# Output gate rows by one matmul with ones, a PSUM bank moved in stage 1, and new costs in the order's planner

## The chip, the cores and the metric

The kernel runs on one core of one Trainium2 chip. The metric is the device time of one execution in microseconds (us); lower is better. Engines are named as in the profile: PE (TensorE), DVE (VectorE), ACT (ScalarE), POOL (GpSimd, which here only issues DMAs) and SP (SyncE, which issues the weight loads).

## What is computed

One layer of a diffusion backbone in float32, with 256 latent tokens, 256 context tokens and a model width of 4096. All weight matrices are read once from DRAM. Shortened from the reference:

```python
shift_x, scale_x, gate_x = modulation(c, w_ada[l], b_ada[l])      # silu(c) @ w_ada + b_ada, 3 x 4096
shift_c, scale_c, gate_c = modulation(c_ctx, w_ada[l], b_ada[l])
h_x = rmsnorm(x, norm_w[l]) * (1.0 + scale_x[:, None]) + shift_x[:, None]
h_c = rmsnorm(ctx, norm_w[l]) * (1.0 + scale_c) + shift_c
q_x, k_x, v_x, ga_x, xl_x, gl_x = jnp.split(h_x @ w_in[l], SPLITS, axis=-1)
q_c, k_c, v_c, ga_c, xl_c, gl_c = jnp.split(h_c @ w_in[l], SPLITS, axis=-1)
# attention of 16 query heads over 512 keys (4 kv heads, QK norm, rotary positions)   -> att_x
# convolution of width 4, gates, one scan per direction over 16 blocks of 128 channels -> lru_x
mix_x = jnp.concatenate([rmsnorm(att_x, out_norm_att[l]) * jax.nn.silu(ga_x),
                         rmsnorm(lru_x, out_norm_lru[l]) * jax.nn.silu(gl_x)], axis=-1)
x_new = x + gate_x[:, None] * (mix_x @ w_out[l])
```

The change concerns `gate_x`, the output gate: 4096 numbers, one for each output column, that multiply the output projection.

## The kernel before

**Arithmetic.** A large matrix product is three float32r matmuls: each operand is split into a rounded high part and the rest. ACT casts a weight tile to its high part (L688, `hi`), DVE subtracts to get the low part (L692, `lo`), and PE does high by high, low by high and high by low (L789 to L791 in stage 1, L1007 to L1009 after). A piece is two weight rows of 128, so six matmuls of 128x128 by 512 columns. There are seven raw weight slots (`raw`), three `hi` and three `lo` slots.

**Stage 1** goes over the 32 tiles of 128 input channels in groups of 1, 1, 2, 2, 2 and then 4. For each group the modulation (shift and scale of both streams) is made from `w_ada`, partly by PE (`on_tensor`, L525) and partly by DVE (`on_vector`, L515, two products for each weight row of 128), then turned (`coeff_tasks`, a bank of class `pe`). The token tiles are transposed by PE into a `pe` bank (`turn`, L639), and ACT reads that bank four times to make high part and full value (`modulate`, L649 and L650); DVE makes the low part from the single `ta` buffer. Then come the columns that both streams need, key, value and recurrence input, in six blocks of 512 columns. The four token tiles (two latent, two context) of a block fill one PSUM bank each, of class `pm`; when a group is through a block, DVE adds each bank to an SBUF accumulator (L809) and the bank is free. The eight banks of PSUM are four `pm`, two `pe`, one `pt`, one `po`.

**Stage 2** makes the query blocks, attention, the recurrence and the two SiLU gates, **stage 3** the output projection in eight chunks of 512 columns, each multiplied by its gate and added to `x` by DVE and stored by POOL's queue. `Q0` is the end of stage 1 and `O0` the start of stage 3; a chunk (`CH`) is 192 large matmuls.

**Output gate.** Row j covers 512 columns. DVE adds 32 products of a weight row with a column of `silu(c)` in one accumulator `ga` (L914; L912 for the first one), so that each partition holds a partial sum. For rows 0 to 3 four matmuls with a column of ones (L927) sum over partitions into four columns of `gT`, DVE adds the bias (L931), and in stage 3 four matmuls with the identity (L1518) and an ACT copy (L1522) spread them again over 128 partitions. Rows 4 to 7 have the bias as one row of the first addend (L921, L922), are summed and spread by one matmul with a matrix of ones (L937, `spread`), and ACT copies them to an SBUF tile (L942, `keep`).

**Order.** Tiles are placed by hand. Each step is a task with an engine, a cost, what it depends on and which buffers it takes and frees. A planner (`Plan`) simulates the engines with those costs and so fixes one order for all; each engine's queue then follows it strictly. POOL's DMAs are one in-order queue in the plan (engine "S"), SP's weight loads are issued in the order in which they are used, as slots come free. A cost or a bank count that is changed in the plan therefore re-deals the order everywhere.

Of the kernel before, what the change touches and what calls it, by code (L numbers as in the profile page):

```python
# [55 lines left out]
PICK = 0.10  # L56
MOD_VPOS = 2.7
NCONST = 128 + 2 + 4 * 128


class Task:


    def __init__(self, fn, ops, deps=(), pos=0.0, nb=None, loads=(), frees=0, acq=(), rel=()):
        self.fn, self.ops, self.deps = fn, ops, [d for d in deps if d is not None]
        self.pos, self.nb, self.loads, self.frees = pos, nb, loads, frees
        self.acq, self.rel = acq, rel
        self.start = self.end = self.arrived = None
# [10 lines left out]
def pe(n, k=1):  # L79
    return k * n / 2400  # L80
# [12 lines left out]
class Plan:  # L93
# [23 lines left out]
    def estimate(self, t):  # L117
        s = self.t[t.ops[0][0]]
        for d in t.deps:
            s = max(s, d.end + (0.0 if d.ops[-1][0] == t.ops[0][0] else self.LAT[d.ops[-1][0]]))  # L120
        need = {}
        for n in t.acq:
            need[n] = need.get(n, 0) + 1
        for n, c in need.items():
            f = sorted(self.free[n])
            if len(f) < c:
                return None
            s = max(s, f[c - 1] + 0.1)
# [90 lines left out]
def kernel(  # L219
# [34 lines left out]
    SLOTS = dict(h4=(22, 1024), a8=(6, 2048), raw=(RAW, 1024), hi=(HL, 1024), lo=(HL, 1024), tp=(TP, 512), ta=(1, 512), wg=(2, 514),  # L254
                 xin=(1, 512), u=(1, 512), ga=(1, 512), ab=(2, 16), cf=(1, 16), mx=(3, 2), ss=(5, 16), pm=(4, 512), pe=(2, 512), pt=(1, 512), po=(1, 512))
    ROUNDED = ("h4", "hi", "lo")
# [69 lines left out]
    epsc = cp.tile([128, 1], F32, name="epsc")  # L326
    ones_c = cp.tile([128, 1], F32, name="ones_c")
    par_t = slot("xin", [128, 512])
# [12 lines left out]
    V.memset(pick[:, 3:4], 1.0)  # L341
    V.memset(ones_c, 1.0)
    V.memset(par[:, 0], 0.0)
# [20 lines left out]
    rope = {}  # L364
    gT = cp.tile([128, KT], F32, name="gT")
    st = cp.tile([128, 4, NG], F32, name="st")
# [310 lines left out]
    def unit(w_l, k0, kw, c0, cw, pos):  # L677

        u = len(units)
        shape = [128, kw, cw]  # L680
        src = w_l[128 * k0 : 128 * (k0 + kw), c0 : c0 + cw].rearrange("(k p) n -> p k n", p=128)
        d = dict(pos=pos)
        units.append(d)

        def high(raw):
            d["raw"] = raw
            d["hi"] = slot("hi", shape, F32R)
            S.copy(d["hi"], raw)  # L688

        def low():  # L690
            d["lo"] = slot("lo", shape, F32R)
            V.tensor_tensor(out=d["lo"], in0=d["raw"], in1=d["hi"].bitcast(F32), op=ALU.subtract)  # L692
            drop(d["raw"])

        before = units[u - 1] if u else {}
        p = pos - AHEAD
        d["high"] = add(high, [("A", act(1024))], [before.get("high")], p, nb=pos - 40, loads=[(shape, src)], acq=["hi"])
        d["low"] = add(low, [("D", dve(1024))], [d["high"], before.get("low")], p, frees=1, acq=["lo"])
        return u
# [31 lines left out]
    def accum_task(name, tile_, fn, dep, pos):  # L731
# [3 lines left out]
        deps = [dep, summed.get((name, tile_)), acc_last.get(name)]  # L735
        acc_last[name] = summed[name, tile_] = add(fn, ops, deps, pos, acq=acq, rel=["pm"])

# [160 lines left out]
    WHOLE = 4  # L898
    gbias, wide = {}, {}

    def gate_tasks(j, prev, lru_read=None):

        d = {}
        src = w_ada[0, :, 2 * D + 512 * j : 2 * D + 512 * j + 512].rearrange("(p k) n -> p k n", p=128)

        def mul(w, k):
            if k == 0:
                d["acc"] = slot("ga", [128, 512])
            for i in range(2):
                s_ = sc[:, 0, k + i : k + i + 1]  # L910
                if k + i == 0 and j < WHOLE:
                    V.tensor_scalar_mul(d["acc"], w[:, i], s_)  # L912
                else:
                    V.scalar_tensor_tensor(out=d["acc"], in0=w[:, i], scalar=s_, in1=d["acc"] if k + i else gbias["row"], op0=ALU.mult, op1=ALU.add)  # L914
# [24 lines left out]

        def keep():  # L940
            gb = h4t([128, 512])
            S.copy(gb, d["pg"])  # L942
            drop(d["pg"])
            wide[j] = gb

        if j >= WHOLE:
            if j == WHOLE:
                prev = add(row, [("D", 0.3)], [lru_read, prev], gate_pos(16 * j) - 8, acq=["xin"])
            else:
                prev = add(row, [("S", 0.05, 6.0)], [prev], gate_pos(16 * j) - 1)  # L950
        for k in range(0, KT, 2):
            pos = gate_pos(16 * j + k // 2)
            prev = add(lambda w, k=k: mul(w, k), [("D", 1.33)], [prev], pos, nb=pos - GATE_EARLY, loads=[([128, 2, 512], src[:, k : k + 2])], frees=1,
                       acq=["ga"] if k == 0 else [])
        if j >= WHOLE:
            a = add(spread, [("P", 1.05)], [prev], pos, acq=["pe"], rel=["ga"])
            gate_fin.append(add(keep, [("A", act(512))], [a], pos, acq=["h4"], rel=["pe"]))
            return prev
        a = add(sums, [("P", 0.8)], [prev], pos, acq=["pe"], rel=["ga"])
        gate_fin.append(add(fin, [("D", 0.1)], [a], pos, rel=["pe"]))  # L960
        return prev

# [5 lines left out]

    gated = None
    for j in range(WHOLE):  # L970
        gated = gate_tasks(j, gated)

# [73 lines left out]

    ROTATE = dve(128, 4) + dve(512, 2)
    res = {}
# [419 lines left out]
    def make_post():  # L1468
# [20 lines left out]
    for n in range(NB):  # L1489
        prev = lru_tasks(n, Q0 + 0.9 * CH + span * n, span, prev)  # L1490
    for j in range(WHOLE, 8):
        gated = gate_tasks(j, gated, prev["cv"])

# [12 lines left out]
    for j in range(8):  # L1506
# [6 lines left out]

        def turn(d=d, j=j):
            d["pg"] = bank()
            for i in range(4):
                n = 4 * j + i
                T.matmul(d["pg"][:, 128 * i : 128 * i + 128], gT[:, n : n + 1].to_broadcast([128, 128]), ident, start=True, stop=True)  # L1518

        def put(d=d):  # L1520
            d["gb"] = slot("tp", [128, 512])
            S.copy(d["gb"], d["pg"])  # L1522
            drop(d["pg"])

        def scaled(t, d=d, j=j):
            o = d["ps"][t]
            if j >= WHOLE:
                d["gb"] = wide[j]
            for c in (slice(0, 256), slice(256, 512)) if j == 7 else (slice(0, 512),):
# [12 lines left out]
        if j < WHOLE:  # L1542
            a = add(turn, [("P", pe(2048))], [gb], p + 0.85 * CH, nb=p + 0.5 * CH, acq=["pe"])
            gb = add(put, [("A", act(512))], [a], p + 0.87 * CH, acq=["tp"], rel=["pe"])
        d["ps"], ends = rows_pieces(o_units[j], mh, lambda g: [mixed[g]])
        for t in range(2):
            a = add(lambda t=t, f=scaled: f(t), [("D", dve(512, 2))], [ld, gb, ends[t]], p + CH, rel=["pm"] + ([["tp"], ["h4"]][j >= WHOLE] if t else []))
            add(lambda t=t, f=store: f(t), [("S", 0.73)], [a], p + CH, rel=["a8"] if t else [])
# [51 lines left out]
```

## Time and profile before

| | |
|---|---|
| median of 3 runs | 1749.03 us (1748.51 to 1751.44) |
| the profiled execution | 1748.74 us |
| its span | 1747.0 us |
| PE busy | 1694.0 us, 97% of the span |
| PE weight load busy | 1305.3 us, 75% |
| DVE busy | 1393.2 us, 80% |
| ACT busy | 854.0 us, 49% |
| DMA | 451.23 MB, 258 GB/s in the mean |
| large matmuls | 768 of each line in stage 1, 1280 of each line after |

Times in the trace are from the start of the span. Of PE, the start times tell more than the busy time: matmuls are pipelined and their records overlap. An "idle before" in brackets at a row is the time its engine had been without work, and who ended it. Stage 1's large matmuls start from 34.5 to 706.8 us, those of stages 2 and 3 from 707.5 to 1740.8 us.

### The profile page before, as it was taken

The numbers are of one execution on the slowest core, as the hardware profiler recorded it, in microseconds if no ns is written. First come the engines' busy times: TensorE is split into PE (matmuls) and PEld (weight loads), VectorE is DVE, ScalarE is ACT, GpSimd is POOL, SyncE is SP. The second block draws the span as 40 slices with busy tenths as digits, with TensorE's granted clock in tenths as the row PEclk, the third lists the DMA queues.
The fourth block names the chain that finished last, engine by engine and source line by source line (L and its number), as shares of the span: only waits on it lengthen the run. The fifth ranks groups of instructions, "written<-read, shape, count | busy, mean of one in ns | idle before, by whom it ended". The sixth has DMA issues, their size and how long they took to land.

```text
span 1747.0 us, 22544 instructions
## 1 busy us (share of the span) xinstructions
PE 1694.0 (97%) x8133; PEld 1305.3 (75%) x8133; DVE 1393.2 (80%) x1998; ACT 854.0 (49%) x1254; POOL 60.5 (3%) x97
## 2 busy tenths in 40 slices
PE   4999999999999999999999999999999999999998
PEld 2556677777676778877777778888888788888887
DVE  2368888898988897597886779989987988786874
ACT  5422232232323233366886877777687643343332
POOL 0000000000000000000000000000000000000000
PEclk9999999999999999999999999999999999999999
DMA  9999988889787875885544538767876799898983
GB/s 320 333 354 327 352 297 279 298 298 318 249 319 276 284 254 164 269 260 185 189 127 125 153 119 294 219 222 232 266 237 202 225 338 324 289 327 284 332 290 103
DMA packets 253104, 451.23 MB, mean 258 GB/s; under 512 B 14976, under 2 KB 56560, under 8 KB 252480
## 3 DMA queue, kind: packets, MB, share of 16 engines
q1 hardware_dynamic: 246624, 428.43, 73.9%
q0 software_dynamic: 6368, 21.36, 3.5%
q8 instruction: 64, 1.05, 0.2%
q14 instruction: 48, 0.39, 0.1%
HBM read 441.34 MB, written 8.39 MB: 257 GB/s over the span
## 4 chain that ended last, share of the span: by engine, by line
PE 56%; DVE 23%; DMA 10%; issue 5%; ACT 5%; SPq 1%; DVEq 0%; ACTq 0%
PE pm L1009 11%; PE pm L1007 11%; PE pm L1008 11%; DMA raw<-in_w_ada_dram 8%; DVE lo L692 7%; PE pm L789 5%; PE pm L790 5%; PE pm L791 5%; DVE u L515 3%; DVE xin L515 2%; ACT hi L688 2%; DMA raw<-in_w_in_dram 2%; DVE ga L914 1%; DVE a L809 1%; PE pt L525 1%
## 5 line engine op out<-in xcount | busy, mean ns | idle before, releaser
L688 ACT CAST hi<-raw 128x1024 fp32r<-128x1024 f32 x416 | 435.6, 1050 | 684.8 <-PE pm L1009 284.0
L692 DVE TENSOR_TENSOR lo<-raw,hi 128x1024 fp32r<-128x1024 f32 x416 | 506.6, 1221 | 178.5 <-ACT hi L688 175.8
L1007 PE MATMUL pm<-hi,h 128*128 128x512 f32 x1280 | 514.8, 402 | 0.0
L1008 PE MATMUL pm<-lo,h 128*128 128x512 f32 x1280 | 499.4, 390 | 2.0 <-DVE lo L692 1.9
L1009 PE MATMUL pm<-hi,h 128*128 128x512 f32 x1280 | 499.6, 390 | 0.0
L789 PE MATMUL pm<-hi,h 128*128 128x512 f32 x768 | 313.8, 409 | 9.1 <-DVE a L809 7.7
L790 PE MATMUL pm<-lo,h 128*128 128x512 f32 x768 | 301.5, 393 | 0.8 <-DVE lo L692 0.8
L791 PE MATMUL pm<-hi,h 128*128 128x512 f32 x768 | 301.5, 393 | 0.0
L1008 PEld LDWEIGHTS pm<-lo,h 128*128 128x128 f32 x1280 | 240.8, 188 | 55.8 <-issue 5.3
L1007 PEld LDWEIGHTS pm<-hi,h 128*128 128x128 f32 x1280 | 240.6, 188 | 52.2 <-issue 5.3
L1009 PEld LDWEIGHTS pm<-hi,h 128*128 128x128 f32 x1280 | 240.4, 188 | 50.7
L789 PEld LDWEIGHTS pm<-hi,h 128*128 128x128 f32 x768 | 145.0, 189 | 82.1 <-issue 28.9
L914 DVE SCALAR_TENSOR_TENSOR ga<-raw,sc,ga 128x512 f32<-128x512 f32 x248 | 185.8, 749 | 5.6 <-DMA raw<-in_w_ada_dram 0.8
L791 PEld LDWEIGHTS pm<-hi,h 128*128 128x128 f32 x768 | 145.1, 189 | 31.6
L790 PEld LDWEIGHTS pm<-lo,h 128*128 128x128 f32 x768 | 145.4, 189 | 27.6 <-DVE lo L692 1.3
L809 DVE TENSOR_TENSOR a<-pm,a 128x512 f32<-128x512 f32 x202 | 133.0, 686 | 35.4 <-PE pm L791 35.1
L515 DVE SCALAR_TENSOR_TENSOR xin<-raw,sc,xin 128x512 f32<-128x512 f32 (+1 forms) x188 | 135.7, 722 | 24.6 <-DMA raw<-in_w_ada_dram 24.6
L515 DVE SCALAR_TENSOR_TENSOR u<-raw,sc,u 128x512 f32<-128x512 f32 (+1 forms) x188 | 135.8, 722 | 0.0
L525 PE MATMUL po<-raw,wg 128*32 128x256 f32 (+2 forms) x560 | 55.9, 473 | 26.1 <-DMA raw<-in_w_ada_dram 26.0
L525 PEld LDWEIGHTS po<-raw,wg 128*32 128x32 f32 x560 | 15.6, 120 | 55.1 <-DMA raw<-in_w_ada_dram 21.9
L649 ACT ACTIVATE ta<-pe,ab 128x256 f32<-128x256 f32 x64 | 36.1, 564 | 42.4 <-PE pe L639 31.1
L525 PE MATMUL pt<-raw,wg 128*32 128x512 f32 (+2 forms) x456 | 42.8, 466 | 4.1 <-DMA raw<-in_w_ada_dram 3.9
(198 smaller groups left out, 1295.4 us busy)
## 6 DMA issues: line engine op xcount, KB each, us to landing
raw<-in_w_ada_dram SPq DMA_DIRECT2D x384, 512.0 KB, 5.9
raw<-in_w_in_dram SPq DMA_DIRECT2D x288, 512.0 KB, 4.6
raw<-in_w_out_dram SPq DMA_DIRECT2D x128, 512.0 KB, 5.1
h<-in_x_dram SPq DMA_DIRECT2D x8, 512.0 KB, 7.9
h<-in_ctx_dram SPq DMA_DIRECT2D x8, 512.0 KB, 10.1
xl_d<-a POOLq DMA_DIRECT2D x4, 1024.0 KB, 5.9
xin<-xl_d POOLq DMA_DIRECT2D x16, 256.0 KB, 4.8
a<-in_x_dram POOLq DMA_DIRECT2D x8, 512.0 KB, 6.2
```

What stands on the lines that cost most here:

```text
L515: V.scalar_tensor_tensor(out=a, in0=d["w"][:, i], scalar=s_, in1=a, op0=ALU.mult, op1=ALU.add)
L525: T.matmul(d["ps"][32 * q : 32 * q + 32, :], sc32[half][:, o : o + 32], ws[i // step][:, i % step], start=(part, quad) == first_p, stop=(p ...
L688: S.copy(d["hi"], raw)
L692: V.tensor_tensor(out=d["lo"], in0=d["raw"], in1=d["hi"].bitcast(F32), op=ALU.subtract)
L789: T.matmul(ps[s, t], hi, wh, start=f, stop=False)
L790: T.matmul(ps[s, t], hi, wl, start=False, stop=False)
L791: T.matmul(ps[s, t], lo, wh, start=False, stop=e)
L809: V.tensor_tensor(out=a, in0=ps[s, t], in1=a, op=ALU.add)
L914: V.scalar_tensor_tensor(out=d["acc"], in0=w[:, i], scalar=s_, in1=d["acc"] if k + i else gbias["row"], op0=ALU.mult, op1=ALU.add)
L1007: T.matmul(ps[t], hi, wh, start=f, stop=False)
L1008: T.matmul(ps[t], hi, wl, start=False, stop=False)
L1009: T.matmul(ps[t], lo, wh, start=False, stop=e)
```

## The change

1. The class `pm` has five banks and `pe` one. When the last sums of stage 1 are done, a task without an instruction (`hand_over`) gives one bank from `pm` to `pe`, so stages 2 and 3 have four and two as before.
2. The plan adds 0.6 us (`SUM_LAG`) to the time at which a sum may follow its matmuls. The cast (`high`), the gate product and the rotation get other costs (1.05 for 0.94, 1.42 for 1.33, 0.47 more).
3. All eight gate rows start with a clear of `ga` and the bias row by DMA into its first partition; 32 equal products follow. All are summed by one matmul with ones.
4. Rows 0 to 3: ACT copies one partition of the sum back to `ga`, POOL stores it in DRAM (`away`), and the buffer is free when that has landed. In stage 3 POOL loads it on all partitions into an `h4` slot (`back`). `gT`, `turn` and `put` are gone.
5. The gate tasks enter the plan after the recurrence, not ahead of the unit lists.

```diff
+SUM_LAG = 0.6
...
-            s = max(s, d.end + (0.0 if d.ops[-1][0] == t.ops[0][0] else self.LAT[d.ops[-1][0]]))
+            s = max(s, d.end + (0.0 if d.ops[-1][0] == t.ops[0][0] else self.LAT[d.ops[-1][0]] + t.lag))
...
-                 ... ss=(5, 16), pm=(4, 512), pe=(2, 512), pt=(1, 512), po=(1, 512))
+                 ... ss=(5, 16), pm=(5, 512), pe=(1, 512), pt=(1, 512), po=(1, 512))
...
-        d["high"] = add(high, [("A", act(1024))], [before.get("high")], p, nb=pos - 40, loads=[(shape, src)], acq=["hi"])
+        d["high"] = add(high, [("A", 1.05)], [before.get("high")], p, nb=pos - 40, loads=[(shape, src)], acq=["hi"])
...
-        acc_last[name] = summed[name, tile_] = add(fn, ops, deps, pos, acq=acq, rel=["pm"])
+        acc_last[name] = summed[name, tile_] = add(fn, ops, deps, pos, acq=acq, rel=["pm"], lag=SUM_LAG)
...
+        def clear():
+            d["acc"] = slot("ga", [128, 512])
+            V.memset(d["acc"], 0.0)
+
         def row():
-            if j == WHOLE:
-                gbias["row"] = slot("xin", [128, 512])
-                V.memset(gbias["row"], 0.0)
-            Q.dma_start(gbias["row"][0:1], b_ada[0:1, 2 * D + 512 * j : 2 * D + 512 * j + 512])
+            Q.dma_start(d["acc"][0:1], b_ada[0:1, 2 * D + 512 * j : 2 * D + 512 * j + 512])
-        def sums():
-            d["pg"] = bank()
-            for i in range(4):
-                T.matmul(d["pg"][:, i : i + 1], d["acc"][:, 128 * i : 128 * i + 128], ones_c, start=True, stop=True)
-            drop(d["acc"])
-        def fin():
-            V.tensor_tensor(out=gT[:, 4 * j : 4 * j + 4], in0=d["pg"][:, 0:4], in1=b_ga[:, 4 * j : 4 * j + 4], op=ALU.add)
-            drop(d["pg"])
         def spread():
             d["pg"] = bank()
             T.matmul(d["pg"], post["ones"], d["acc"], start=True, stop=True)
+            if j >= WHOLE:
+                drop(d["acc"])
+        def keep():
+            if j < WHOLE:
+                S.copy(d["acc"][0:1], d["pg"][0:1])
+            else:
+                wide[j] = h4t([128, 512])
+                S.copy(wide[j], d["pg"])
+            drop(d["pg"])
+        def away():
+            Q.dma_start(g_d[j : j + 1], d["acc"][0:1])
             drop(d["acc"])
...
+        prev = add(clear, [("D", 0.3)], [prev], pos - 0.6, nb=pos - GATE_EARLY, acq=["ga"])
+        prev = add(row, [("S", 0.05, 6.0)], [prev], pos - 0.5)
         for k in range(0, KT, 2):
-            prev = add(lambda w, k=k: mul(w, k), [("D", 1.33)], [prev], pos, ...)
+            prev = add(lambda w, k=k: mul(w, k), [("D", 1.42)], [prev], pos, ...)
+        a = add(spread, [("P", 1.05)], [prev, post["made"]], pos, acq=["pe"], rel=["ga"] if j >= WHOLE else [])
+        a = add(keep, [("A", act(512))], [a], pos, acq=["h4"] if j >= WHOLE else [], rel=["pe"])
+        if j < WHOLE:
+            a = add(away, [("S", 0.05, 4.0)], [a], pos, rel=["ga"])
...
-    ROTATE = dve(128, 4) + dve(512, 2)
+    ROTATE = dve(128, 4) + dve(512, 2) + 0.47
...
+    def hand_over():
+        f = free["pm"].pop(0)
+        free["pe"].append((clock[0], f[1] + 10, f[2]))
+    handed = add(hand_over, [("P", 0.0)], [acc_last[n] for n, _ in BLOCKS], Q0 - 1, acq=["pm"], rel=["pe"])
...
-        def turn(d=d, j=j):
-            ...
-        def put(d=d):
-            ...
+        def back(j=j):
+            wide[j] = h4t([128, 512])
+            Q.dma_start(wide[j], g_d[j : j + 1].to_broadcast([128, 512]))
...
-            a = add(turn, [("P", pe(2048))], [gb], p + 0.85 * CH, nb=p + 0.5 * CH, acq=["pe"])
-            gb = add(put, [("A", act(512))], [a], p + 0.87 * CH, acq=["tp"], rel=["pe"])
+            gb = add(back, [("S", 0.4, 6.0)], [gb], p + 0.5 * CH, nb=p + 0.35 * CH, acq=["h4"])
```

## Rows read from the trace of the kernel before

**Rows 1.** The page, part 1: busy time, share of the span, instructions.
```profile
PE 1694.0 (97%) x8133; PEld 1305.3 (75%) x8133; DVE 1393.2 (80%) x1998; ACT 854.0 (49%) x1254; POOL 60.5 (3%) x97
```

**Rows 2.** Busy time by stretch: us, busy (x) by engine, PEclk, DMA share, GB/s.
```profile
34.00:160.00 126.00, 118.32 (x825) 69.79 (x825) 75.57 (x141) 50.77 (x104) 3.92 (x8) 0.99 1.06 344
...
320.00:480.00 160.00, 156.43 (x762) 113.70 (x761) 141.24 (x214) 45.66 (x65) 0.00 (x0) 1.00 0.87 297
...
480.00:640.00 160.00, 155.56 (x728) 115.48 (x727) 143.31 (x217) 46.97 (x68) 0.00 (x0) 1.00 0.83 284
...
1200.00:1300.00 100.00, 99.45 (x451) 81.01 (x450) 96.94 (x126) 70.61 (x86) 6.50 (x9) 1.00 0.81 265
...
1366.00:1747.00 381.00, 375.67 (x1667) 309.82 (x1667) 286.66 (x312) 151.17 (x150) 13.78 (x23) 1.00 0.83 283
```

**Rows 3.** Waits: us in total, times, longest us.
```profile
PE pm L789 <- DVE a L809: 7.7, 9, 1.4
...
PE pt L1109 <- DVE tp L1044: 1.5, 5, 0.5
...
DVE a L809 <- PE pm L791: 35.1, 29, 4.3
...
POOL wg L1256 <- DVE lo L1289: 292.9, 14, 24.4
```

**Rows 4.** Timeline, first stage: start us, us, engine, line, operation, idle before.
```profile
451.74 0.39 PE L789 MATMUL pm<-hi,h 128*128 128x512 f32 x1
...
452.19 0.39 PE L791 MATMUL pm<-hi,h 128*128 128x512 f32 x1
...
452.42 0.75 DVE L515 SCALAR_TENSOR_TENSOR u<-raw,sc,u 128x512 f32<-128x512 f32 x1
...
453.08 0.69 DVE L809 TENSOR_TENSOR a<-pm,a 128x512 f32<-128x512 f32 x1
...
453.92 0.47 PE L789 MATMUL pm<-hi,h 128*128 128x512 f32 x1 [1.34 <-DVE a L809]
```

**Rows 5.** Timeline of PE: one gate row summed, one turned, one spread.
```profile
744.94 0.95 PE L927 MATMUL pe<-ones_c,ga 128*128 128x1 f32 x8
745.75 0.48 PE L1007 MATMUL pm<-hi,h 128*128 128x512 f32 x1
...
1424.31 1.05 PE L1518 MATMUL pe<-con,gT 128*128 128x128 f32 x8
1425.12 0.48 PE L1007 MATMUL pm<-hi,h 128*128 128x512 f32 x1
...
1438.85 1.02 PE L937 MATMUL pe<-ga,a 128*128 128x512 f32 x2
1439.31 0.79 PE L1007 MATMUL pm<-hi,h 128*128 128x512 f32 x1
1439.94 0.39 PE L1008 MATMUL pm<-lo,h 128*128 128x512 f32 x1
```

**Rows 6.** Groups of VectorE by line: busy us, mean ns, idle before.
```profile
L914 DVE SCALAR_TENSOR_TENSOR ga<-raw,sc,ga 128x512 f32<-128x512 f32 x248 | 185.8, 749 | 5.6 <-DMA raw<-in_w_ada_dram 0.8
...
L912 DVE TENSOR_SCALAR ga<-raw,sc 128x512 f32<-128x512 f32 x4 | 1.9, 482 | 0.0
...
L921 DVE MEMSET xin<- 128x512 f32 x1 | 0.5, 485 | 0.1
```

**Rows 7.** Timeline of two transposes of the modulation in sequence, first stage.
```profile
385.28 0.60 PE L639 MATMUL pe<-con,h 128*128 128x128 f32 x4
...
387.11 0.60 PE L639 MATMUL pe<-con,h 128*128 128x128 f32 x4
...
387.28 0.57 ACT L650 ACTIVATE h<-pe,ab 128x256 fp32r<-128x256 f32 x1
```

**Rows 8.** DMA issues: KB each, median us to landing.
```profile
xin<-in_b_ada_dram POOLq DMA_DIRECT2D x4, 2.0 KB, 5.1
...
u<-in_shape_consts_dram POOLq DMA_DIRECT2D x2, 256.0 KB, 4.5
```

More of the change, by code (lines that the diff above doesn't have):

```diff
@@ L57, with __init__ @@
 MOD_VPOS = 2.7
+SUM_LAG = 0.6
 NCONST = 128 + 2 + 4 * 128
 class Task:
-    def __init__(self, fn, ops, deps=(), pos=0.0, nb=None, loads=(), frees=0, acq=(), rel=()):
+    def __init__(self, fn, ops, deps=(), pos=0.0, nb=None, loads=(), frees=0, acq=(), rel=(), lag=0.0):
         self.fn, self.ops, self.deps = fn, ops, [d for d in deps if d is not None]
         self.pos, self.nb, self.loads, self.frees = pos, nb, loads, frees
-        self.acq, self.rel = acq, rel
+        self.acq, self.rel, self.lag = acq, rel, lag
         self.start = self.end = self.arrived = None
@@ L254 @@
     SLOTS = dict(h4=(22, 1024), a8=(6, 2048), raw=(RAW, 1024), hi=(HL, 1024), lo=(HL, 1024), tp=(TP, 512), ta=(1, 512), wg=(2, 514),
-                 xin=(1, 512), u=(1, 512), ga=(1, 512), ab=(2, 16), cf=(1, 16), mx=(3, 2), ss=(5, 16), pm=(4, 512), pe=(2, 512), pt=(1, 512), po=(1, 512))
+                 xin=(1, 512), u=(1, 512), ga=(1, 512), ab=(2, 16), cf=(1, 16), mx=(3, 2), ss=(5, 16), pm=(5, 512), pe=(1, 512), pt=(1, 512), po=(1, 512))
     ROUNDED = ("h4", "hi", "lo")
@@ L326 @@
     epsc = cp.tile([128, 1], F32, name="epsc")
-    ones_c = cp.tile([128, 1], F32, name="ones_c")
     par_t = slot("xin", [128, 512])
@@ L341 @@
     V.memset(pick[:, 3:4], 1.0)
-    V.memset(ones_c, 1.0)
     V.memset(par[:, 0], 0.0)
@@ L364 @@
     rope = {}
-    gT = cp.tile([128, KT], F32, name="gT")
     st = cp.tile([128, 4, NG], F32, name="st")
@@ L898, with gate_tasks @@
     WHOLE = 4
-    gbias, wide = {}, {}
-    def gate_tasks(j, prev, lru_read=None):
+    wide = {}
+    g_d = drp.tile([WHOLE, 512], F32, name="g_d")
+    def gate_tasks(j, prev):
         d = {}
@@ L906, in mul @@
         def mul(w, k):
-            if k == 0:
-                d["acc"] = slot("ga", [128, 512])
             for i in range(2):
                 s_ = sc[:, 0, k + i : k + i + 1]
[L911 to L914, printed above, removed]
+                V.scalar_tensor_tensor(out=d["acc"], in0=w[:, i], scalar=s_, in1=d["acc"], op0=ALU.mult, op1=ALU.add)
             drop(w)
+        def clear():
+            d["acc"] = slot("ga", [128, 512])
+            V.memset(d["acc"], 0.0)
         def row():
-            if j == WHOLE:
-                gbias["row"] = slot("xin", [128, 512])
-                V.memset(gbias["row"], 0.0)
-            Q.dma_start(gbias["row"][0:1], b_ada[0:1, 2 * D + 512 * j : 2 * D + 512 * j + 512])
-        def sums():
-            d["pg"] = bank()
-            for i in range(4):
-                T.matmul(d["pg"][:, i : i + 1], d["acc"][:, 128 * i : 128 * i + 128], ones_c, start=True, stop=True)
-            drop(d["acc"])
-        def fin():
-            V.tensor_tensor(out=gT[:, 4 * j : 4 * j + 4], in0=d["pg"][:, 0:4], in1=b_ga[:, 4 * j : 4 * j + 4], op=ALU.add)
-            drop(d["pg"])
+            Q.dma_start(d["acc"][0:1], b_ada[0:1, 2 * D + 512 * j : 2 * D + 512 * j + 512])
         def spread():
@@ L937, in spread @@
             T.matmul(d["pg"], post["ones"], d["acc"], start=True, stop=True)
-            drop(d["acc"])
[L940 to L950, printed above, removed]
+            if j >= WHOLE:
[9 more added lines that the diff above has]
+            Q.dma_start(g_d[j : j + 1], d["acc"][0:1])
+            drop(d["acc"])
+        pos = gate_pos(16 * j)
+        prev = add(clear, [("D", 0.3)], [prev], pos - 0.6, nb=pos - GATE_EARLY, acq=["ga"])
+        prev = add(row, [("S", 0.05, 6.0)], [prev], pos - 0.5)
         for k in range(0, KT, 2):
             pos = gate_pos(16 * j + k // 2)
[L953 to L960, printed above, removed]
+            prev = add(lambda w, k=k: mul(w, k), [("D", 1.42)], [prev], pos, nb=pos - GATE_EARLY, loads=[([128, 2, 512], src[:, k : k + 2])], frees=1)
+        a = add(spread, [("P", 1.05)], [prev, post["made"]], pos, acq=["pe"], rel=["ga"] if j >= WHOLE else [])
+        a = add(keep, [("A", act(512))], [a], pos, acq=["h4"] if j >= WHOLE else [], rel=["pe"])
+        if j < WHOLE:
+            a = add(away, [("S", 0.05, 4.0)], [a], pos, rel=["ga"])
+        gate_fin.append(a)
         return prev
@@ L967, in gate_pos @@
         return O0 + (7 * CH + 10) * (i - GATE_S2) / (128 - GATE_S2)
-    gated = None
-    for j in range(WHOLE):
-        gated = gate_tasks(j, gated)
     def unit_rows(w_l, c0, p):
@@ L1490 @@
         prev = lru_tasks(n, Q0 + 0.9 * CH + span * n, span, prev)
-    for j in range(WHOLE, 8):
-        gated = gate_tasks(j, gated, prev["cv"])
+    gated = None
+    for j in range(8):
+        gated = gate_tasks(j, gated)
     for j in range(4):
@@ L1512, in load @@
             Q.dma_start(d["xr"], x[0, :, 512 * j : 512 * j + 512].rearrange("(t p) d -> p t d", p=128))
-        def turn(d=d, j=j):
[L1515 to L1518, printed above, removed]
-        def put(d=d):
-            d["gb"] = slot("tp", [128, 512])
-            S.copy(d["gb"], d["pg"])
-            drop(d["pg"])
+        def back(j=j):
+            wide[j] = h4t([128, 512])
+            Q.dma_start(wide[j], g_d[j : j + 1].to_broadcast([128, 512]))
         def scaled(t, d=d, j=j):
             o = d["ps"][t]
-            if j >= WHOLE:
-                d["gb"] = wide[j]
+            d["gb"] = wide[j]
             for c in (slice(0, 256), slice(256, 512)) if j == 7 else (slice(0, 512),):
@@ L1542 @@
         if j < WHOLE:
-            a = add(turn, [("P", pe(2048))], [gb], p + 0.85 * CH, nb=p + 0.5 * CH, acq=["pe"])
-            gb = add(put, [("A", act(512))], [a], p + 0.87 * CH, acq=["tp"], rel=["pe"])
+            gb = add(back, [("S", 0.4, 6.0)], [gb], p + 0.5 * CH, nb=p + 0.35 * CH, acq=["h4"])
         d["ps"], ends = rows_pieces(o_units[j], mh, lambda g: [mixed[g]])
         for t in range(2):
-            a = add(lambda t=t, f=scaled: f(t), [("D", dve(512, 2))], [ld, gb, ends[t]], p + CH, rel=["pm"] + ([["tp"], ["h4"]][j >= WHOLE] if t else []))
+            a = add(lambda t=t, f=scaled: f(t), [("D", dve(512, 2))], [ld, gb, ends[t]], p + CH, rel=["pm"] + (["h4"] if t else []))
             add(lambda t=t, f=store: f(t), [("S", 0.73)], [a], p + CH, rel=["a8"] if t else [])
```

## Prediction

> **What bounds the kernel now.** I read the page's first part, then the work by stretch, then the waits, then the timeline of TensorE (PE) at the longest of these waits. PE shows as busy for 97% of the span [rows 1], but records of pipelined matmuls overlap: the large ones have 0.39 us each and start 0.226 us apart (451.74 to 452.19 is two steps [rows 4]). So the loss has to be sought in start times that lie further apart than this step. By stretch there are three regimes [rows 2]. From 34 to 160 us the DMA share is above 1 and PE idles for 7.7 us of 126: the weights' arrival sets the pace. In the rest of stage 1 PE idles 3.6 and 4.4 us per 160 us, at a full granted clock, while VectorE (DVE) is busy for 141 and 143 of 160. In stages 2 and 3 PE hardly idles, and there only work taken off PE shortens the run.
>
> Who makes PE idle in stage 1 is in the waits: nine waits of L789, the first matmul of a piece, for L809, the sum of an older bank into SBUF, 7.7 us together and none over 1.4 us [rows 3]. The timeline shows one. The last matmul of a piece starts at 452.19; the next piece wants the bank whose sum runs on DVE only from 453.08, behind a product of the modulation (L515) that started at 452.42; PE goes on at 453.92 [rows 4]. The opposite wait is there too: DVE stands in front of L809 until PE has finished the bank, 29 times and 35.1 us [rows 3]. Four banks are taken by the four token tiles of one column block, so the sum of a tile has about three pieces (18 matmuls, 4.1 us) before its bank is wanted again; DVE is in order, so a sum placed early makes DVE wait and one placed late makes PE wait.
>
> **The change part by part.** The sum is made against the profiled execution, 1748.74 us, which is 0.29 us below the median of the three runs.
>
> *Fifth bank.* A bank more puts one piece, six matmuls or 1.36 us, between the end of a tile and the next use of its bank. The longest wait is 1.4 us, so eight or nine of the nine fit into it. Each costs more than its idle time: 452.19 to 453.92 is 1.73 us where a step is 0.23, so 1.50 us for an idle time of 1.34 [rows 4]; nine times 0.16 on top of 7.7 gives 9.1 us. SUM_LAG puts sums up to 0.6 us later in the order, which eats less than half of the new 1.36 us and takes from the 35.1 us in which DVE stands. Bounds: 0 (the wait comes back as another one) to −9.1; I take −7.3, four fifths, since a sum may slip by one operation more.
>
> *One bank fewer for the rest in stage 1.* Transposes, their sums and the parameters share one bank until the hand-over. A transposition may then start only when ScalarE has read the one before it. In the trace of before this is already so for all but five of 33; the rows show the shape: transposes at 385.28 and 387.11, the fourth read of the first begins at 387.28 and takes 0.57, so it would have waited 0.7 us [rows 7]. Three of the five lie at 233 to 238 us, the whole overlap is 6.5 us by the same subtraction. The planner can put matmul pieces in front of a late transposition, and what comes next (the single `ta` buffer) serialises ScalarE's part anyway. Bounds 0 to +6.5; I take +0.7, near the end without loss because a piece is ready nearly always after 160 us.
>
> *Gate rows.* For rows 0 to 3 two things leave PE: four one-column matmuls (744.94 to the next large matmul at 745.75, 0.81 us) and in stage 3 the four that spread the column (1424.31 to 1425.12, 0.81 us) [rows 5]. One matmul with ones comes in, which rows 4 to 7 show today: 0.46 us to the next large matmul, and that one is followed after 0.63 instead of 0.23, so 0.86 us in all [rows 5]. Net 4 × (0.81 + 0.81 − 0.86) = 3.0 us less on PE, in stages where PE is the limit. Its bounds are close, −2.5 to −3.5. ScalarE exchanges a copy for a copy.
>
> DVE gets seven memsets more at 0.485 us and four products at 0.749 instead of 0.482 [rows 6]: +4.5 us. What hides it is that the gate row has no near deadline and stage 3 has DVE busy for 287 of 381 us [rows 2]. From 1200 to 1300 DVE is at 96.9 of 100 [rows 2]; there the cover is thin, and if the addition fell wholly before stage 3 at the point where its first pieces wait, it would cost up to 4.5 us. I take +0.3.
>
> POOL's queue gets four bias rows more (four are there today, 2 KB, landing after 5.1 us), four stores of a row and four broadcast loads of 256 KB (a load of that size lands after 4.5 us) [rows 8]. The loads are placed half a chunk, some 21 us, ahead of use; cover enough. A gate row now begins only after the store of the one before has landed, a clear and the bias row: about 5 + 0.5 + 5 us of pause in the chain, hidden because other loads and products fill DVE. Taken at 0; without the cover it is the third rival.
>
> *Planner's numbers.* ROTATE, the cast and the gate product get other costs, so queue orders change everywhere. The one wait that bears directly on it: transposes of the queries wait for the rotation, 1.5 us in five waits [rows 3]. With 0.47 us more in the plan, PE does a piece first. Bounds 0 to −1.5, taken −1.0; a re-dealt order elsewhere has no sign I can read.
>
> Sum: −7.3 + 0.7 − 3.0 + 0.3 − 1.0 = −10.3, so 1748.74 − 10.3 = 1738.4; with the 0.29 us to the median, and no more precision than that, 1738 us.
>
> **The rivals.** *DVE is the bound of stage 1.* If DVE's total work and not one late sum holds PE back, the fifth bank only moves the wait to the low halves (L692) or to the modulation. For it: 141 and 143 of 160 us busy [rows 2]. Against it: DVE itself stands 35.1 us in front of sums [rows 3], so it has time to give. It leaves the −3.0 and half of −1.0, about 1745 us. The Trainium skill, "Perfetto Trace Analysis", section "Identifying the Most-Contended Engine", says the same from the other side: occupancy is a fair measure for VectorE, matmul busy time is not one for TensorE. By that rule DVE at 89% would be the engine to relieve; the start-to-start step says PE was full between the waits.
>
> *The missing second bank costs its whole overlap.* Then +6.5 replaces +0.7 and the result is 1744 us. For it: the transposes at 233 to 238 us come three in a row. Against it: 28 of 33 would not notice. "Perfetto Trace Analysis" in the Trainium skill, section "Matmuls", wants independent groups to rotate through different banks so that evacuation overlaps the next group; it speaks for the fifth bank and against the single one, and the trace shows the first need more often (nine waits against none for a `pe` bank).
>
> *POOL's queue stands (slower).* One place: in stage 2 a bias row waits behind the load of a recurrence block, and that queue is known to stand there for up to 24.4 us [rows 3]. The product that needs the row then stops DVE in order. PE lives on the three `lo` buffers, 3 × 12 × 0.226 = 8.2 us; a full stand costs 24.4 − 8.2 = 16.2, giving 1754 us. It decides from a stand of 8.2 + 10.7 = 18.9 us, where the gain of the rest is gone. Against it: the plan holds POOL as one in-order queue and 6 us for the row, against 5.1 measured [rows 8].
>
> A fourth, weaker: the 35.1 us that DVE stands come free and carry stage 1 beyond the nine waits; 1730 us.
>
> **How the numbers follow.** The forecast has 0.50 (its own range 1733 to 1743), the DVE rival 0.20, the bank rival 0.13, POOL 0.13, the larger gain 0.04. A measurement of this kernel can tell about 0.2% (3.5 us) from no change, so the border of faster is 1745.5. Faster: 0.50 + 0.04 + 0.12 (of the DVE rival) + 0.08 (of the bank rival) = 0.74. Same: 0.08 + 0.05 + 0.01 of POOL = 0.14. Slower: 0.12. The range 1732 to 1750 takes in the forecast and the two rivals on its side and leaves out POOL and the larger gain, some 0.17.
>
> **What would show it.** In the profile of the changed kernel: waits of L789's successor for the sum fall from 7.7 to under 2 us; DVE's wait in front of the sum falls well below 35.1; stage 1 ends 6 to 8 us earlier and stages 2 and 3 are together 3 to 4 us shorter; no wait of PE for the transposes' bank above 2 us in all; the four spreads in stage 2 take 0.86 us each. The prediction is wrong if PE's waits turn up under another name in stage 1 (low halves, raw weights), if a product of the gate row is seen to wait for the bias row for more than 8 us, or if the stages keep their lengths although the nine waits are gone.

## The result and the profile after

The changed kernel takes 1734.85 us (median of 3 runs, 1733.89 to 1738.57) against 1749.03; the ratio is 0.9922, 95% interval 0.9901 to 0.9943. Five more runs of it later, beside other kernels, gave 1736.8 us and 0.994 (0.9926 to 0.9954). So it is 0.6 to 0.8% faster, 10 to 14 us, where 11 us were forecast (1738, range 1732 to 1750).

The page's first part and the work by stretch of the changed kernel answer to [rows 1, 2]; columns as there.

```profile
PE 1690.2 (97%) x8077; PEld 1300.8 (75%) x8077; DVE 1397.5 (80%) x2000; ACT 854.0 (49%) x1254; POOL 67.3 (4%) x109
```
```profile
34.00:160.00 126.00, 118.39 (x823) 69.98 (x825) 75.14 (x142) 51.44 (x105) 3.94 (x8) 0.97 1.06 343
320.00:480.00 160.00, 159.39 (x757) 116.61 (x756) 141.23 (x215) 46.38 (x66) 0.00 (x0) 1.00 0.85 290
480.00:640.00 160.00, 157.24 (x748) 116.45 (x747) 146.70 (x221) 47.38 (x67) 0.50 (x1) 1.00 0.87 295
1200.00:1300.00 100.00, 99.88 (x452) 81.78 (x451) 96.45 (x122) 72.97 (x91) 5.85 (x8) 1.00 0.81 266
1366.00:1736.00 370.00, 365.26 (x1606) 300.32 (x1604) 284.54 (x314) 144.72 (x141) 16.02 (x28) 1.00 0.85 294
```

PE idles 0.6 us instead of 3.6 between 320 and 480 us, but 2.8 instead of 4.4 between 480 and 640. DVE has more to do between 480 and 640 (146.7 for 143.3 us) while PE idles less there than before. The waits of the same execution, first those of other engines, then PE's own:

```profile
POOL wg L1241 <- DVE lo L1274: 262.8, 13, 36.4
...
DVE a L807 <- PE pm L789: 19.4, 18, 2.7
```
```profile
PE pm L993 <- DVE lo L690: 3.0, 6, 1.5
PE pm L787 <- DVE a L807: 2.8, 3, 1.4
...
PE pt L1094 <- ACT hi L686: 0.4, 1, 0.4
PE pe L637 <- DVE cf L607: 0.4, 1, 0.4
...
PE pe L637 <- ACT h L648: 0.2, 1, 0.2
```

The wait of PE for a sum (now L787 for L807) fell from 7.7 us in nine places to 2.8 in three; DVE's wait in front of a sum from 35.1 to 19.4 [rows 3]. The wait for the rotation (now L1094) has become one of 0.4 us for ACT. For the single bank of the transposes (L637) PE waited 0.6 us in all. Its wait for low halves in stages 2 and 3 (L993) grew from 1.9 to 3.0 us. A gate row of the first four in stage 2, and the DMAs of the gate:

```profile
741.28 1.02 PE L922 MATMUL pe<-ga,a 128*128 128x512 f32 x2
741.74 0.79 PE L992 MATMUL pm<-hi,h 128*128 128x512 f32 x1
742.37 0.39 PE L993 MATMUL pm<-lo,h 128*128 128x512 f32 x1
```
```profile
h<-g_d POOLq DMA_DIRECT2D x4, 256.0 KB, 7.3
...
ga<-in_b_ada_dram POOLq DMA_DIRECT2D x8, 2.0 KB, 3.2
...
g_d<-ga POOLq DMA_DIRECT2D x4, 2.0 KB, 2.1
```

The matmul with ones takes 0.46 us to the next large matmul, which is followed after 0.63, as in [rows 5]. A broadcast row lands after 7.3 us, a bias row after 3.2. POOL stood in front of a recurrence load for up to 36.4 us and no gate product stood with it: in the whole trace the products of the gate waited 0.8 us, once, for a raw weight.

Where the time went is read from three start times in each trace: the first large matmul of stage 2 (before: 707.74 us), the first of stage 3 (1385.17) and the last of all (1741.51). The table gives the change of the three lengths in us; "sum" is PE's wait for a sum, "front" DVE's wait in front of one. The column "its end" is the part of stage 1's change that comes after its 1729th large matmul (563.6 us before), about where the gate's first task, its clear, now stands in the order (557 us). Each line is one execution: two executions of the changed kernel, with the same order, differ by 4.5 us at the end of stage 1, while stages 2 and 3 agree to 0.1 us.

| kernel | ratio to before (95%) | stage 1 | its end | stage 2 | stage 3 | sum, places | front |
|---|---|---|---|---|---|---|---|
| before | 1 | 0 | 0 | 0 | 0 | 7.7, 9 | 35.1 |
| changed, first trace | 0.9922 (0.9901 to 0.9943) | −3.7 | −3.4 | −2.9 | −3.8 | 2.8, 3 | 19.4 |
| changed, second trace | 0.9940 (0.9926 to 0.9954) | −8.2 | −3.7 | −2.9 | −3.8 | 2.5, 3 | 18.2 |
| bank and later sums alone | 0.9947 (0.9935 to 0.9960) | −10.1 | −1.2 | −0.4 | 0.0 | none | 19.4 |
| bank alone | 1.0005 (0.9994 to 1.0017) | −1.0 | −1.0 | +1.6 | −0.1 | 7.0, 5 | 37.5 |
| later sums alone | 0.9985 (0.9977 to 0.9994) | −2.7 | +0.3 | +1.3 | 0.0 | 1.2, 3 | 21.1 |
| gate rows alone | 0.9938 (0.9926 to 0.9951) | −5.9 | −5.5 | −1.3 | −3.8 | 4.3, 4 | 34.0 |
| cast and rotation costs alone | 0.9965 (0.9952 to 0.9977) | −5.0 | −1.0 | −2.6 | 0.0 | 2.8, 3 | 33.0 |
| cast cost alone | 0.9967 (0.9955 to 0.9979) | −7.2 | −1.2 | −2.3 | 0.0 | 2.5, 2 | 34.5 |
| changed, without bank | 0.9926 (0.9914 to 0.9938) | −7.3 | −5.1 | −3.1 | −3.8 | 2.0, 2 | 20.5 |
| changed, without bank and later sums | 0.9923 (0.9909 to 0.9936) | −6.7 | −3.1 | −3.0 | −3.8 | 2.5, 2 | 34.0 |
| changed, old cast cost | 0.9899 (0.9887 to 0.9911) | −12.7 | −2.8 | −3.8 | −3.8 | none | 20.7 |
| before, order re-dealt (tie window) | 1.0034 (1.0022 to 1.0047) | +4.1 | +0.3 | +0.8 | −0.1 | 3.9, 5 | 36.5 |
| before, order re-dealt (latency) | 1.0047 (1.0031 to 1.0063) | +5.8 | +2.3 | −0.2 | 0.0 | 12.3, 8 | 33.7 |

### The profile page after: what moved, and what is told of

Its sections match the earlier page's. It is cut to its first block, busy times and chain, and to the rows that moved or that the text cites. A ratio compares the mean times of both kernels' runs of the same rounds, so it can differ in the third digit from the quotient of the medians.

```text
span 1736.6 us, 22453 instructions
## 1 busy us (share of the span) xinstructions
PE 1690.2 (97%) x8077; PEld 1300.8 (75%) x8077; DVE 1397.5 (80%) x2000; ACT 854.0 (49%) x1254; POOL 67.3 (4%) x109
## 2 busy tenths in 40 slices
DMA packets 253679, 452.28 MB, mean 260 GB/s; under 512 B 15296, under 2 KB 56880, under 8 KB 253056
## 4 chain that ended last, share of the span: by engine, by line
PE 73%; DVE 11%; DMA 8%; ACT 3%; issue 3%; SPq 1%; DVEq 0%; ACTq 0%
PE pm L993 14%; PE pm L994 14%; PE pm L992 14%; PE pm L787 8%; PE pm L788 7%; PE pm L789 7%; DMA raw<-in_w_ada_dram 7%; DVE lo L690 3%; PE po L523 2%; DVE u L513 2%; PE pt L523 1%; DVE xin L513 1%; ACT hi L686 1%; PE po L1159 1%; DMA raw<-in_w_in_dram 1%
## 5 line engine op out<-in xcount | busy, mean ns | idle before, releaser
L993 PE MATMUL pm<-lo,h 128*128 128x512 f32 x1280 | 499.4, 390 | 3.0 <-DVE lo L690 3.0
L787 PE MATMUL pm<-hi,h 128*128 128x512 f32 x768 | 312.3, 407 | 3.9 <-DVE a L807 2.8
L993 PEld LDWEIGHTS pm<-lo,h 128*128 128x128 f32 x1280 | 240.5, 188 | 58.9 <-DVE lo L690 6.3
L787 PEld LDWEIGHTS pm<-hi,h 128*128 128x128 f32 x768 | 145.1, 189 | 73.0 <-issue 25.3
L908 DVE SCALAR_TENSOR_TENSOR ga<-raw,sc,ga 128x512 f32<-128x512 f32 x256 | 191.8, 749 | 5.8 <-DMA raw<-in_w_ada_dram 0.8
L807 DVE TENSOR_TENSOR a<-pm,a 128x512 f32<-128x512 f32 x202 | 132.4, 684 | 19.4 <-PE pm L789 19.4
L523 PE MATMUL po<-raw,wg 128*32 128x256 f32 (+2 forms) x560 | 54.0, 472 | 25.9 <-DMA raw<-in_w_ada_dram 25.9
L523 PEld LDWEIGHTS po<-raw,wg 128*32 128x32 f32 x560 | 15.5, 119 | 52.8 <-issue 20.0
L523 PE MATMUL pt<-raw,wg 128*32 128x512 f32 (+2 forms) x456 | 46.4, 473 | 3.9 <-DMA raw<-in_w_ada_dram 3.9
```

What stands on the lines that cost most here:

```text
L523: T.matmul(d["ps"][32 * q : 32 * q + 32, :], sc32[half][:, o : o + 32], ws[i // step][:, i % step], start=(part, quad) == first_p, stop=(p ...
L787: T.matmul(ps[s, t], hi, wh, start=f, stop=False)
L807: V.tensor_tensor(out=a, in0=ps[s, t], in1=a, op=ALU.add)
L993: T.matmul(ps[t], hi, wl, start=False, stop=False)
```

## The experiments

The first theory was the prediction's: the bank removes nine waits, the gate rows take 3 us off PE. The rival that the parts alone raised is that the order which the planner happens to deal decides.

**1. Bank, hand-over and later sums alone**, on the kernel before:

```diff
+SUM_LAG = 0.6
-... pm=(4, 512), pe=(2, 512), ...
+... pm=(5, 512), pe=(1, 512), ...
+    handed = add(hand_over, ...)
-        acc_last[name] = ... add(fn, ops, deps, pos, acq=acq, rel=["pm"])
+        acc_last[name] = ... add(fn, ops, deps, pos, acq=acq, rel=["pm"], lag=SUM_LAG)
```

> The kernel before with the fifth bank in stage 1, the hand-over and the later sums alone (0.6 us); gate rows and all other costs as before. The bank theory (nine waits of PE for a sum are the loss): 5 to 8 us faster, ratio near 0.9962, all of it at the end of stage 1 and kept to the end; PE's wait for the sum falls from 7.7 to 3 us or less. The order theory (what the planner happens to deal, and not the bank, made the gain): the wait falls too, but the end moves by anything within +-4 us, since the lead is lost in stage 2. The DVE theory (VectorE bounds stage 1): at most 2 us, and waits for the low halves or raw weights grow by what the sums lost.

1739.34 us, ratio 0.9947. Stage 1 is 10.1 us shorter, no wait of PE for a sum is left, and the lead is kept to the end (10.5 us at the last matmul). DVE's wait in front of sums:

```profile
DVE a L810 <- PE pm L792: 19.4, 17, 4.5
```

This is the mechanism as predicted. Before, the steps across the nine waits took 9.2 us more from start to start than nine plain steps, and none of that is left. Whether the size exceeds the bound of 9.1 us cannot be told: the medians give 8.5 us, the trace 10.5.

**2. Gate rows alone**: the changed kernel with

```diff
-SUM_LAG = 0.6
+SUM_LAG = 0.0
-... pm=(5, 512), pe=(1, 512), ...
+... pm=(4, 512), pe=(2, 512), ...
-    handed = add(hand_over, ...)
-        d["high"] = add(high, [("A", 1.05)], ...)
+        d["high"] = add(high, [("A", act(1024))], ...)
-            prev = add(lambda w, k=k: mul(w, k), [("D", 1.42)], ...)
+            prev = add(lambda w, k=k: mul(w, k), [("D", 1.33)], ...)
-    ROTATE = dve(128, 4) + dve(512, 2) + 0.47
+    ROTATE = dve(128, 4) + dve(512, 2)
```

> The gate rows of the changed kernel (one matmul with ones, DRAM, biases among the addends) on four and two banks, no later sums, old costs. Work theory: 3.0 to 3.8 us faster (ratio 0.998), as four times the 0.8 to 0.9 us that four spreads in stage 3 took on PE; the matmul with ones in stage 2 costs what the four column matmuls did. Order theory: the -3 to -4 us are in stage 3 as well, but stage 2 moves by up to 4 us either way.

1737.89 us, ratio 0.9938. Stage 3 is 3.8 us shorter, as every kernel with the new gate rows shows. But stage 1 is 5.9 us shorter as well, where the gate has no PE work and its first products start only at 614 us; the three waits for sums between 606 and 618 us are gone. The work theory does not hold for that part. The traces show where it arises: up to 568 us PE's order is that of the kernel before, and 5.5 of the 5.9 us come at about that point or later, where the gate's tasks are dealt differently.

**3. Cast and rotation costs alone** on the kernel before, the same instructions:

```diff
-        d["high"] = add(high, [("A", act(1024))], ...)
+        d["high"] = add(high, [("A", 1.05)], ...)
-    ROTATE = dve(128, 4) + dve(512, 2)
+    ROTATE = dve(128, 4) + dve(512, 2) + 0.47
```

> The kernel before with the planner's numbers for the cast (1.05) and the rotation (+0.47) alone; the same instructions in another order. Prediction's term: 1.0 us faster (0 to 1.5), from PE's waits of 1.5 us for the rotation. Order theory: anything within +-4 us, and the stretches that move have nothing to do with the rotation.

1741.15 us, ratio 0.9965: 6.6 us where the term was 1.0, with 5.0 of the trace's 7.6 in stage 1, which rotates nothing but two key tiles at its end.

**4. The changed kernel without the stage 1 part**:

```diff
-SUM_LAG = 0.6
+SUM_LAG = 0.0
-... pm=(5, 512), pe=(1, 512), ...
+... pm=(4, 512), pe=(2, 512), ...
-    handed = add(hand_over, ...)
```

> The changed kernel with four and two banks throughout and sums without the 0.6 us; gate rows and costs as changed. Bank theory: it loses 5 to 8 of the changed kernel's gain, so 1741 to 1743 us when before is 1749, ratio near 0.9965. Order theory: it keeps most of the gain, ratio near 0.993. PE's wait for the sum is back at 7 to 10 us in either.

1735.1 us, ratio 0.9923: it loses nothing. So each part alone shortens stage 1 by 5 to 10 us, and together they don't add up. The column "its end" sorts them: all six lines with the new gate rows gain 2.8 to 5.5 us there, the others between −1.2 and +2.3; up to that point the gate rows alone change nothing (−0.4). At that point the order theory led.

**5. The changed kernel once more**, no edit, for a second trace.

> The changed kernel once more, beside the others, for a second trace. If its small gain in stage 1 (3.7 us at its end, where the bank and the later sums alone had 10.1) belongs to its order, stage 1 ends again at 703 to 705 us; if a slow execution made it, it ends near 700, and the early loss of 4 us at 198 us is gone. Time 1733 to 1738.

1736.8 us. Stage 1 now ends 8.2 us earlier than before and not 3.7, so 4.5 us of what the first trace lacked was that execution's; a loss of 1.9 us at 198 us stayed. The stretch of its middle, to be set beside [rows 2] (there 156.43 and 155.56 of 160):

```profile
320.00:640.00 320.00, 317.34 (x1514) 234.50 (x1513) 289.66 (x436) 93.83 (x134) 0.49 (x1) 1.00 0.86 293
```

**6. The changed kernel without the bank**, later sums kept:

```diff
-... pm=(5, 512), pe=(1, 512), ...
+... pm=(4, 512), pe=(2, 512), ...
-    handed = add(hand_over, ...)
```

> The changed kernel with four and two banks throughout, later sums kept. Bank theory: sums that come 0.6 us later without a fifth bank make PE wait more, 10 to 14 us, and the kernel is 8 to 12 us slower than the changed one, about 1744. Order theory: the plan knows of four banks and places its sums accordingly; within 4 us of the changed kernel, 1733 to 1739.

1734.21 us, ratio 0.9926: the bank can go without loss when the other parts are there.

**7 and 8. Two orders without an aim**, on the kernel before. `PICK` is the window in us in which the planner prefers the more urgent of two ready tasks, `LAT` its latency between engines:

```diff
-PICK = 0.10                                  # experiment 7
+PICK = 0.12
-LAT = dict(P=0.2, A=0.14, D=0.14, S=0.15)    # experiment 8
+LAT = dict(P=0.21, A=0.14, D=0.14, S=0.15)
```

> The kernel before with nothing changed but the window in which the planner takes the more urgent of two ready tasks (0.12 for 0.10 us): the same instructions and banks, an order dealt anew, with no aim. Order theory: the order before is a poor one of many, so a new one is 2 to 10 us faster; the waits for sums change too. Bank and work theories: no reason for a gain, within 3 us of before.

> The kernel before with the plan's latency of a TensorE result at 0.21 for 0.20 us and nothing else: a second order without an aim. Order theory: 2 to 10 us faster than before. Bank and work theories: within 3 us of before. The two together tell how far a deal alone moves this kernel.

1752.88 and 1754.98 us, both slower, by 0.34 and 0.47%. That fells the plain form of the order theory: the order before was not a bad draw that any other would better. It also gives the size of a draw, that is of what a new order alone changes: stage 1 moved by 4 to 6 us for nothing. In the first the waits for sums fell to 3.9 us, but from the start of a modulation matmul (L525, L538) to PE's next start it took 116.3 us in all (110.2 before); in the second the waits grew:

```profile
PE pm L789 <- DVE a L809: 12.3, 8, 3.2
```

**9. The fifth bank alone**: experiment 1 with

```diff
-SUM_LAG = 0.6
+SUM_LAG = 0.0
```

> The kernel before with the fifth bank, the single bank for the rest and the hand-over; sums as early in the plan as before. Bank theory: nearly all of the 10 us that bank and later sums gave together, so 1737 to 1740, with PE's wait for sums under 2 us and VectorE's wait in front of sums still near 35. Plan theory (what helps is that the plan no longer believes a sum can follow its matmuls at once): at most half of it, 1742 or more, with waits for sums left above 3 us. Two orders without an aim were 6 and 8 us slower than before, so a deal by itself is no reason to expect a gain.

1749.16 us, ratio 1.0005: nothing. The waits in this kernel (L790 is the first matmul of a piece, L810 the sum), then DVE and PE at the longest:

```profile
DVE a L810 <- PE pm L792: 37.5, 31, 4.3
...
PE pm L790 <- DVE a L810: 7.0, 5, 2.8
```
```profile
451.80 0.76 DVE L516 SCALAR_TENSOR_TENSOR xin<-raw,sc,xin 128x512 f32<-128x512 f32 x1
452.47 0.76 DVE L516 SCALAR_TENSOR_TENSOR u<-raw,sc,u 128x512 f32<-128x512 f32 x1
453.13 0.76 DVE L516 SCALAR_TENSOR_TENSOR xin<-raw,sc,xin 128x512 f32<-128x512 f32 x1
453.79 0.77 DVE L516 SCALAR_TENSOR_TENSOR u<-raw,sc,u 128x512 f32<-128x512 f32 x1
454.45 0.70 DVE L810 TENSOR_TENSOR a<-pm,a 128x512 f32<-128x512 f32 x1
```
```profile
452.05 0.39 PE L792 MATMUL pm<-hi,h 128*128 128x512 f32 x1
455.21 0.65 PE L790 MATMUL pm<-hi,h 128*128 128x512 f32 x1 [2.77 <-DVE a L810]
```

Four modulation products run ahead of the sum at 454.45; the piece that would have followed at 452.28 starts at 455.21. Before, such a wait was at most 1.4 us, now 2.8. It is not this place alone. Take the 124 sums of the groups of four and the time from the start of a bank's last matmul to the start of its sum: over 5 us it was for 10 sums before (the longest 7.7 us), for 18 now (10.1), for none in experiment 1 (4.9). The bank was there and the order used it up.

**10. The later sums alone**: experiment 1 with

```diff
-... pm=(5, 512), pe=(1, 512), ...
+... pm=(4, 512), pe=(2, 512), ...
-    handed = add(hand_over, ...)
```

> The kernel before with sums 0.6 us later in the plan, four and two banks. Bank theory: nothing to hold a later sum, PE's wait for sums rises above the 7.7 us of before, time 1747 or more. Plan theory: VectorE's wait in front of sums halves (35 to 20 or less), PE's wait falls below 4, 4 to 9 us faster. A loss of 2 us between 155 and 198 us is expected of either, as in the three orders with the lag.

1745.28 us, ratio 0.9985. DVE's wait in front of sums and PE's wait for them:

```profile
DVE a L810 <- PE pm L792: 21.1, 19, 3.2
```
```profile
PE pm L790 <- DVE a L810: 1.2, 3, 0.8
```

Both fell, on four banks. Only 2.7 us of it are left at the end of stage 1.

**11. The cast's cost alone**, on the kernel before:

```diff
-        d["high"] = add(high, [("A", act(1024))], ...)
+        d["high"] = add(high, [("A", 1.05)], ...)
```

> The kernel before with the plan's cost of the cast at 1.05 us (measured: 1.05) for 0.94 and nothing else. Plan theory: it gives the stage 1 part of what the two costs gave together, 4 to 6 us at the end of stage 1, with PE's wait for sums below 4 us; stage 2 keeps its length, since the 2.6 us there belong to the rotation's cost. Deal theory: within 3 us of before or slower, as with the two orders without an aim.

1742.64 us, ratio 0.9967, stage 1 shorter by 7.2 us with two waits left (below). PE's order in stage 1 is the same as in experiment 3, so this is that draw once more, not a second one; and the profiled execution (1739.37 us) was the fastest of five, the median gains 5.3 us in all. Stage 2 also lost 2.3 us, so the rotation's cost is not needed for what shortened it in experiment 3.

```profile
PE pm L789 <- DVE a L809: 2.5, 2, 1.9
```

**12. The changed kernel with the old cast cost**:

```diff
-        d["high"] = add(high, [("A", 1.05)], ...)
+        d["high"] = add(high, [("A", act(1024))], ...)
```

> The changed kernel with the cast's cost as before (0.94), all else changed. If parts add up by stage: 10 us in stage 1 (bank and later sums with the old cast), 2.9 in stage 2, 3.8 in stage 3, so 1730 to 1732 and 3 to 5 us faster than the changed kernel. If the parts of stage 1 are three ways to remove the same waits, it is within 3 us of the changed kernel, 1733 to 1738.

1730.36 us, ratio 0.9899 (0.9887 to 0.9911): the fastest of all. Up to about 560 us PE's order is that of experiment 1, and experiment 1 is then 8.9 us ahead of before and this kernel 9.9. The interval lies clear of the changed kernel's second measurement (0.9926 to 0.9954) and overlaps the first (0.9901 to 0.9943) by 0.001. PE between 320 and 640 us is busy for 319.70 of 320, against 156.43 + 155.56 = 311.99 before:

```profile
320.00:640.00 320.00, 319.70 (x1526) 237.28 (x1525) 289.12 (x436) 93.56 (x133) 0.50 (x1) 1.00 0.86 296
```

## Why the prediction was right, point by point

**The total** was right: 1738 forecast, 1734.85 measured, faster by 14.2 us in the first runs and 10.3 in the second where 11 were said. That it fits so well is in part luck. The largest term, the bank's −7.3, is not what the changed kernel gained by: without the bank, or without bank and later sums, it is no slower (experiments 6 and 4). In its place, what comes with the new gate rows (at the end of stage 1 and in stage 3) and the 2.9 us of stage 2 were larger than said. Of the signs named, PE's waits for sums fell to 2.8 and 2.5 us and not under 2, stage 1 ended 3.7 and 8.2 us earlier where 6 to 8 were said, and stages 2 and 3 are 6.7 us shorter, not 3 to 4; DVE's wait, the transposes' bank and the spreads came as said, and PE's waits for low halves in stage 1 stayed at 0.8 us.

**Fifth bank, −7.3.** Nine waits as the loss of stage 1: right; where they are all gone (experiments 1 and 12) stage 1 is 10 and 13 us shorter. The step that failed is "the longest wait is 1.4 us, so eight or nine of the nine fit into it". It took the order as given. The planner knows the bank and deals so that the sum may come later by as much: alone the bank left 7.0 us of waits and gained nothing. SUM_LAG, which the prediction counted as eating into the bank's gain, is the other half: it reserves the time that the plan did not know of. Bank alone −1.0, lag alone −2.7, both −10.1 us in stage 1; by the medians +1.2, −2.7 and −8.5 us in all. The timeline of experiment 1 near the place of experiment 9 shows two modulation products, not four, between sums:

```profile
445.41 0.74 DVE L516 SCALAR_TENSOR_TENSOR u<-raw,sc,u 128x512 f32<-128x512 f32 x1
446.07 1.22 DVE L693 TENSOR_TENSOR lo<-raw,hi 128x1024 fp32r<-128x1024 f32 x1
447.21 1.28 DVE L810 TENSOR_TENSOR a<-pm,a 128x512 f32<-128x512 f32 x2
448.41 0.74 DVE L516 SCALAR_TENSOR_TENSOR xin<-raw,sc,xin 128x512 f32<-128x512 f32 x1
449.07 0.75 DVE L516 SCALAR_TENSOR_TENSOR u<-raw,sc,u 128x512 f32<-128x512 f32 x1
449.73 1.28 DVE L810 TENSOR_TENSOR a<-pm,a 128x512 f32<-128x512 f32 x2
```

That the planner spends a slack which it is told of and keeps one which it is not is argued from these orders; no run looked into the plan itself. In the changed kernel nine sums again come later than 5 us, the longest after 9.6 us (9.5 in its second trace, 5.9 without the bank): there the order uses the bank up in spite of the lag.

**The plan's costs, −1.0.** The prediction saw "no sign I can read" in the rest of the order; the cast's cost alone gave 0.33%, mostly in stage 1. It is the measured duration (1.05 us), and waits for sums fell from nine to two. Two aimless draws went the other way, but one cost value is one draw, and its 4 to 6 us at 560 us (experiments 3 and 11, one order) are not clear of what a draw moved for nothing (3.4 and 3.8 us, slower): that the true duration is the reason is not shown. Why it is better with the old banks and worse together with the bank and the later sums (experiment 12 against the changed kernel) stays open. The rotation's waits went from 1.5 us to none, as said; its share of stage 2's −2.9 cannot be told from that of the other parts: the cast's cost alone gives −2.3, and without it (experiment 12) stage 2 is 3.8 us shorter.

**Gate rows, −3.0.** Right in mechanism, small in size: −3.8 us, all in stage 3, and outside the bounds of −2.5 to −3.5. The term took 0.81 us for a spread back; the step to the second large matmul after it is longer too, 0.32 us after the row at 1425.12 [rows 5], and each of the four chunks without it was 0.92 to 0.99 us shorter:

```profile
1425.44 0.39 PE L1008 MATMUL pm<-lo,h 128*128 128x512 f32 x1
```

The term counted that second step for the matmul with ones (0.63 us) and not for the narrow ones. With 0.09 us more for each of them it is 4 × (0.90 + 0.90 − 0.86) = 3.8. In stage 2 one matmul with ones costs what four narrow ones did. Not foreseen at all: the 2.8 to 5.5 us at the end of stage 1, in all six lines with the new gate rows. In experiment 2, 3.7 of the 5.5 us are the three waits for sums that are gone, start to start. Whether the rows themselves or their later place in the plan (item 5 of the change) do it was not run apart, nor was the new cost of the gate product; that stays open.

**One bank fewer, +0.7.** 0.6 us of waits: right. (The trace of before has 32 such transpositions, not 33; the five overlaps and their 6.5 us are as said.) What was not foreseen: between the 289th and the 433rd large matmul (155 to 198 us before) all kernels with the later sums need 44.3 to 45.9 us, all without them 42.1 to 43.0, bank or not. The lag costs about 2 us there.

**The rivals.** VectorE does not bound stage 1: with the same work PE gained 10 us and DVE's wait in front of sums halved. The rule of the Trainium skill, "Perfetto Trace Analysis", section "Identifying the Most-Contended Engine", that occupancy names the engine to relieve would have sent us to DVE, busy for 141 of 160 us against 114 of PE's weight loads [rows 2]. The runs differ from it: in experiment 12 DVE is busier than before (289.12 of 320 us for 284.55) where PE lost nearly nothing, so order and slack decided. The bank rival (+6.5) did not come. POOL stood longer than before (36.4 us, and the rival asked for 18.9), but no bias row was late for it. The time of the larger gain, given 0.04, is reached by experiment 12 (1730.36), though not its mechanism alone: 7.6 of the 20.3 us of that trace lie in stages 2 and 3, and DVE still stands for 20.7 us in front of sums.

## What to carry to other kernels

Where a planner deals the order, a resource that the plan knows of is spent by the plan; here the bank helped only together with 0.6 us of reserve put into the plan, and several parts removed the same waits, so parts measured alone do not add up. It pays to compare the orders of two traces first: they show up to which point two kernels are the same, and so which difference can belong to the change. Before a gain of half a per cent is put down to a cause, deal the order anew once or twice without an aim: here that alone moved the time by 0.3 to 0.5%. Work taken off the bound engine where it never idles comes back in full, and can be read from start to start of the neighbours, two steps on.

## What was not expected of the hardware

Two executions of one program, with the same order on PE and DVE, differed by 4.5 us at the end of stage 1 and by less than 0.1 us in the length of what followed. The difference lies in the steps with the modulation's matmuls: from the start of one (L523, L536) to PE's next start it took 113.8 us in all in the one and 109.8 in the other. Only 1.0 us of the 4.5 had come by 156 us, in the stretch where weights set the pace (DMA share 1.06 and 1.07 from 34 to 160 us); the rest came in single steps of 0.4 to 1.0 us up to 590 us, at a DMA share of 0.84 to 0.88. In the largest of these, at 351 us, PE's weight loads stood for raw weights twice, for 1.20 and 1.22 us against 0.60 and 1.11. Why the weights landed later in one execution is not shown.
